# The second half of an mLSTM's token-major values through five PSUM banks instead of two

## The chip, the cores and the metric

One core of a Trainium2 chip (trn2) runs the whole kernel in one launch. The metric is the time of one execution in device microseconds (us), as the median of several runs. The engines are named as the profile names them: PE is TensorE (matmuls; PEld its weight loads), DVE VectorE, ACT ScalarE, POOL GpSimd, SP the engine that issues most DMAs (SPq is its queue). Every engine works through its instructions in the order in which they are put down for it and waits on semaphores.

## What is computed

The reference is one inference step of a hybrid encoder layer over 1152 tokens: 1024 of a prompt and 8 running streams of 16 (nine tiles of 128). A pre-RMSNorm and one input projection give the mLSTM's q, k, v and gates, the attention's q, k, v and gate, and two merge gates. Cut to what matters here:

```python
z = jnp.einsum("btd,de->bte", h, w_in) + b_in
points = [int(p) for p in np.cumsum(IN_WIDTHS)[:-1]]
mq, mk, mv, mo, mz, mi, mf, ... = jnp.split(z, points, axis=-1)
qk = silu(causal_conv(mq, mk))          # q and k of the mLSTM
v = mv.reshape(B, T, M_HEADS, M_HEAD_DIM)   # four heads of 128
h_m = chunkwise mLSTM of q, k, v and the gates, then RMSNorm
u_m = einsum(h_m * silu(mz), w_bm); u_a = einsum(h_a * silu(az), w_ba)
x + einsum(sigmoid(gm) * u_m + sigmoid(ga) * u_a, w_out)
```

The change concerns `v` of heads 2 and 3, the second half of `mv`.

## The kernel before

Every projection is a product of float32 operands split into a rounded high part and a rest, so each step along the 1024 inputs is three matmuls: high by high, high by low and low by high (`mm3`, lines 113 to 116; lines 114, 115 and 116 of the profile are all such matmuls, whatever they compute). Eight such steps (KD = 8) accumulate in one PSUM bank, 24 matmuls for a tile. Most projections are feature-major (`feature_chunk`, line 118): weights stationary, 384 tokens moving, three chunks for a tile of 128 features. The values are token-major (`mv_half`, line 230): 128 tokens stationary, 256 columns moving, one tile for each of the nine token tiles.

The eight PSUM banks of this part are two of the pool `pmain` (tag `pm`), through which all projections go in turn, and one each for the tags `mK`, `mD`, `mS`, `mB`, `mA`, `mH` of the pool `pM` (`pp`). `mK` holds the transposes of `gate_rows`; the other five are used by `mlstm_head` (lines 418 to 532).

`mv_half(1)` comes after `gate_rows()` (the exponential gates' stabilisers, small DVE and ACT work on `gscr` tiles) and `head_inputs(0)` (the projection and the causal convolution of q and k of head 0). For each token tile i it does 24 matmuls into `ps`, one DVE add of the bias into `vt` (line 243), and two DMAs of `vt` to the scratch `v_sc` in HBM (line 245). `vt` has two buffers, so the add of tile i waits until the DMAs of tile i-2 have landed; `pm` has two, so the matmuls of tile i wait for the add of tile i-2:

```python
ps = pmain.tile([P, 512], F32, tag="pm", name="pm")
for k in range(KD):
    mm3(ps[:, :n], hs(k, i), (w_hi[:, k, :n], w_lo[:, k, :n]), k == 0, k == KD - 1)
vt = m1.tile([P, 2, P], F32, tag="vt", name="vt")
dve.tensor_tensor(out=vt.rearrange("p h d -> p (h d)"), in0=ps[:, 0:256], in1=bv[:, 0:256], op=ALU.add)
for j in range(2):
    sp.dma_start(v_sc[2 * half + j][:, i, :], vt[:, j, :])
```

In the text the nine tiles of the second half are t0 to t8. After them PE goes on with `gate_unit(0)`: three chunks through `pm`, emptied by ACT into `go` (line 331). Ahead of the first of these, ACT and DVE split the eight slices of the attention's first weights (`load_wq(a["wq"][0])`, line 145 with `split`, lines 99 and 100: ACT writes `w_hi`, DVE `w_lo`), which take the place of the values' weights; their DMAs (line 144) have four buffers `wqr`.

The instructions' order on each engine is set by the framework's scheduler, which simulates a timeline when the program is built and places an instruction where the simulation finds its operands and buffers free. So DVE's order around the values mixes the adds of line 243 with the splits of weights (`wl`, line 100), the convolution of head 0 (`qT` and `kT`, line 382; silu with a table of ACT in line 384 and the product in line 385), the stabilisers (lines 294 to 324) and decay terms of head 0 that run ahead (`dx`, line 478, from `Mb`, line 420, which is read back from the scratch `M_sc`, line 319).

Of the kernel before, what the change touches and what calls it, by code (L numbers as in the profile page):

```python
# [6 lines left out]
F32 = mybir.dt.float32  # L7
# [7 lines left out]
P = 128  # L15
NT = 9
NPT = 8
T = NT * P
# [11 lines left out]
def emit(tc, a, o, ctx):  # L30
# [29 lines left out]
    pmain = keep("pmain", bufs=2, space=PSUM)  # L60
# [12 lines left out]
    ones = cp.tile([P, P], F32, name="ones")  # L73
# [15 lines left out]
    def rsqrt(y, v, t):  # L89
        """y = v ** -0.5: a guess from the exponent, then Newton steps"""  # L90
        dve.tensor_scalar(out=y.bitcast(I32), in0=v.bitcast(I32), scalar1=-0.5, scalar2=1597463007.0, op0=ALU.mult, op1=ALU.add)
        for _ in range(3):
            newton(y, v, t)
# [41 lines left out]

# [1 line left out]
    esQ, wq_ = open_pool("wq", side="right")  # L137
# [10 lines left out]

# [1 line left out]
    es0, x0 = open_pool("x0", bufs=3, side="left")  # L150
    esp0, px0 = open_pool("px0", bufs=2, space=PSUM)
    # norm_g on all partitions
    gr = x0.tile([1, 1024], F32, name="gr", bufs=1)
    sp.dma_start(gr, a["norm_g"])
    gb = px0.tile([P, 1024], F32, name="gb", bufs=1)
    for _ in range(4):  # TensorE gets up to its clock while the input arrives
        mm(gb[:, 0:P], ones, ones, start=True, stop=True)
    for q in range(2):
        mm(gb[:, q * 512:(q + 1) * 512], ones[0:1, :], gr[:, q * 512:(q + 1) * 512], start=True, stop=True)
    for i in range(NT):  # L160
# [9 lines left out]
        ss, v, r, tt = (st[:, q:q + 1] for q in range(4))  # L170
# [16 lines left out]
    def silu_evac(n, dst_of):  # L187
        """dst = silu(ps + bias) = (tanh(z / 2) + 1) * (z / 2)"""
        def ev(c, ps):
            dst = dst_of(c)  # L190
            t_ = stg.tile([P, CH], F32, tag="th", name="th")
            act.activation(out=dst, in_=ps, func=AF.Identity, scale=0.5, bias=bh[:, n:n + 1])
            act.activation(out=t_, in_=dst, func=AF.Tanh)
            dve.scalar_tensor_tensor(out=dst, in0=t_, scalar=1.0, in1=dst, op0=ALU.add, op1=ALU.mult)
        return ev

    def g_evac(j):
        """tanh(z / 2) of a merge gate (0..7 of the mLSTM branch, 8..15 of the attention branch), to scratch"""
        def ev(c, ps):
            t_ = stg.tile([P, CH], F32, tag="th", name="tg")  # L200
            act.activation(out=t_, in_=ps, func=AF.Tanh, scale=0.5, bias=bh[:, 20 + j:21 + j])
            sp.dma_start(tg_sc[j][:, c * CH:(c + 1) * CH], t_)
        return ev

# [1 line left out]
    esPS, pp = open_pool("pM", bufs=1, space=PSUM)  # L206
# [7 lines left out]
    class Scratch:  # L214
        """small tiles cut from buffers that are in use only later"""
        parts = []
# [13 lines left out]
    def mv_half(half):  # L230
        n = 264 if half == 0 else 256
        if half:
            load_wq(a["wv1"], n)
        bv = m1.tile([P, 264], F32, tag="bv", name="bv", bufs=1)
        sp.dma_start(bv[:, :n], rowb(a["bv"][264 * half:264 * half + n], n))
        if half == 0:
            mv_half.G = gscr(P, 2, 36)
        for i in range(NT):
            ps = pmain.tile([P, 512], F32, tag="pm", name="pm")
            for k in range(KD):  # L240
                mm3(ps[:, :n], hs(k, i), (w_hi[:, k, :n], w_lo[:, k, :n]), k == 0, k == KD - 1)
            vt = m1.tile([P, 2, P], F32, tag="vt", name="vt")
# [3 lines that stand above are left out]
            if half == 0:  # L246
                dve.tensor_tensor(out=mv_half.G[:, :, 4 * i:4 * i + 4], in0=ps[:, 256:264].rearrange("p (s h) -> p s h", s=2),
                                  in1=bv[:, 256:264].rearrange("p (s h) -> p s h", s=2), op=ALU.add)

    def gate_rows():  # L250
        """rows (tile, head) on partitions, tokens of the tile along the columns"""
        G = mv_half.G
# [10 lines left out]
        t1, bb, aa, A = gscr(36, P), gscr(36, P), gscr(36, P), gscr(36, P)  # L263
# [7 lines left out]
        dve.tensor_tensor_scan(out=A, data0=rs[:, 1, :], data1=aa, initial=0.0, op0=ALU.add, op1=ALU.max)  # L271
        # the running stabiliser across the chunks of the prompt: everything on one partition
        pg = pp.tile([P, 512], F32, tag="mK", name="pg")
# [20 lines left out]
        dve.tensor_copy(out=ml[0:32, :], in_=pg[0:32, 128:130])  # L294
        # the running streams: one chunk per stream
        sl = slice(32, 36)
# [8 lines left out]
        sp.dma_start(DEC, rowb(dec_sc, 64))  # L305
        # A becomes M
        pr = slice(0, 32)
# [18 lines left out]
    def gate_unit(h):  # L326
        """4 sigmoid(o) silu(z) / 2 of a head"""
        go = m1.tile([P, T], F32, tag="go", name="go", bufs=1)
# [31 lines left out]
    def conv_part(nt, out, eng):  # L360
        """out [128, T] = silu(conv(u)), the last rows of u to the conv outputs"""
        w = load_nt(a["wn"][nt], eng=pool if nt in (0, 4) else dve)
# [35 lines left out]

    # the attention part's first operands
    load_wq(a["wq"][0], CH)  # L400
# [17 lines left out]
    def mlstm_head(h, qT, kT):  # L418
# [10 lines left out]
        def state(g):  # L429
            """the memory after each chunk of the group"""  # L430
            V1 = V[g] = m2.tile([P, 3, 129], F32, tag="V1", name="V1", bufs=3)
# [114 lines left out]

# [1 line left out]
    esB, bp_ = open_pool("attnP", bufs=2, side="right")  # L548
# [3 lines left out]
    def softmax(pS, nk, bias):  # L552
        """normalised softmax of pS + bias, [128, nk]"""
        pt = ap_.tile([P, 640], F32, tag="prob", name="prob")
# [19 lines left out]
    def qk_transposes(zd):  # L574
        """psum [128, 2, 128]: q and k, the pair's two heads one after the other along the partitions"""
        px = pp.tile([P, 512], F32, tag="pX", name="pX")
        zf = zd.rearrange("p g d -> p (g d)")
        for c in range(2):
            pe.transpose(px[:, c * P:(c + 1) * P], zf[:, c * P:(c + 1) * P], ident)
        return px[:, 0:256].rearrange("p (c t) -> p c t", c=2)  # L580

    # placed in the order of first use, so that the first ones land where the mLSTM part is done first
    shapes = {"za": ([P, T], F32), "Kst": ([P, 2, TP], F32R), "Vst": ([P, NPT, 2, P], F32R),
# [39 lines left out]

    # The order of TensorE's work in this part is set here: the chains of the attention (threads) run as soon as what
    # they wait for should be there, the projections fill the time between. Times are estimates in ns; they decide
    # the order alone.
    class Line:
# [30 lines left out]
    def attend(p, i):  # L658
# [8 lines left out]
        line.now += 2 * PT_NS  # L667
        # hi and lo of a key one above the other, q twice, values as [hi | lo]
        q_hi = bp_.tile([P, 2, P], F32R, tag="q_hi", name="q_hi")
# [58 lines left out]
        for j in range(2):  # L728
# [6 lines left out]
            sPT.give(line.now)  # L735
        # sum of the four partial products of both heads, gated
        sb = ap_.tile([64, 512], F32, tag="pvs", name="pvs", bufs=1)
# [11 lines left out]

    # q of the running streams: two streams per column group, on the partitions of their keys  # L750
    QB = spl.tile([P, 2, 4, 32], F32, name="QB")
# [95 lines left out]
    def tile_work():  # L847
        """gates of the merge and, as soon as a pair's turn comes, its gate z"""
        p = 0
# [38 lines left out]

# [1 line left out]
    def load_ops(src, k0):  # L890
# [7 lines left out]
    def um_evac(j):  # L898
        """2 sigmoid(g_m) u_m, to scratch"""
        def ev(c, ps):  # L900
# [7 lines left out]
    def run_line():  # L908
        chains = [[attend(p, i) for i in range(NPT)] for p in range(4)]
        # at most two tiles of the prompt and the running streams of one pair are under way  # L910
        queue = [c for p in range(4) for c in chains[p]]
# [53 lines left out]

# [1 line left out]
    esF, fp = open_pool("fin", bufs=2, side="right")  # L967
# [3 lines left out]
    for j in range(8):  # L971
        # the projections' weights are done with
        sa = f(wq_.tile([P, KD, CH], F32R, tag=("w_hi", "w_lo")[j % 2], name="sa", bufs=1)).rearrange("p k c -> p (k c)")
# [28 lines left out]

# [1 line left out]
def layout(x):  # L1004
# [106 lines left out]
```

## Time and profile before

| | |
|---|---|
| median of 3 runs | 1077.2 us (1076.9 to 1082.35) |
| profiled execution: span from first to last instruction | 1075.1 us |
| PE busy | 1055.1 us (98%), 7078 matmuls |
| DVE / ACT / POOL busy | 658.3 / 421.3 / 241.4 us (61 / 39 / 22%) |
| mean granted PE clock | 0.998 of full speed |
| DMA | 131.58 MB, mean 122 GB/s |

Of the profiled execution the profile holds the span alone; the median is 2.1 us above it. All times in the rows below are us from the start of that span. A matmul's row gives a start and a duration; matmuls overlap in the array, so the distance from start to start is what one costs in a row of them, and the duration is longer. A row may end in brackets: how long the engine was idle before it, and what ended that.

### The profile page before, as it was taken

What the parts mean: (1) busy time and instruction counts of PE and PEld (TensorE: products, weight loads), DVE (VectorE), ACT (ScalarE), POOL (GpSimd) and SP (SyncE); (2) the same over time, 40 slices, a digit from 0 to 9 for tenths busy, and PEclk for the clock granted to TensorE, in tenths of its full rate; (3) what the DMA queues carried; (4) which work ended last, traced back from release to release, by engine and by line L of the source; (5) the groups of instructions that cost most, each with busy time, mean ns of one, the idle gap of its engine ahead of it and who ended that gap; (6) DMA issues with size and microseconds to landing.
All of it is one profiled execution on the core that took longest, in us unless ns stands there. A gap on an engine that the chain in (4) does not pass through costs nothing.

```text
span 1075.1 us, 19715 instructions
## 1 busy us (share of the span) xinstructions
PE 1055.1 (98%) x7078; PEld 1024.3 (95%) x7078; DVE 658.3 (61%) x1931; ACT 421.3 (39%) x976; POOL 241.4 (22%) x406
## 2 busy tenths in 40 slices
PE   7997999999999999999999999999999999999998
PEld 6997999999999999999999999999999999999998
DVE  6754244775847768877878688878753253573221
ACT  6441243443443215554455456544454330231100
POOL 3000000110202224434432343334322000351000
PEclk9999999999999999999999999999999999999999
DMA  8533333273523444323343244124322387663442
GB/s 241 161 88 61 101 66 53 87 121 101 116 85 127 151 146 167 117 76 111 114 126 99 62 148 137 54 71 141 111 79 84 111 262 243 202 223 106 136 143 67
DMA packets 115664, 131.58 MB, mean 122 GB/s; under 512 B 28197, under 2 KB 91885, under 8 KB 115566
## 3 DMA queue, kind: packets, MB, share of 16 engines
q1 hardware_dynamic: 108654, 120.88, 38.3%
q10 hardware_dynamic: 6912, 9.44, 2.5%
q8 instruction: 56, 0.92, 0.4%
q14 instruction: 42, 0.34, 0.1%
HBM read 96.84 MB, written 33.44 MB: 121 GB/s over the span
## 4 chain that ended last, share of the span: by engine, by line
PE 88%; DMA 6%; DVE 3%; ACT 1%; issue 1%; SPq 1%; POOL 0%; DVEq 0%; ACTq 0%
PE pm L114 24%; PE pm L116 24%; PE pm L115 24%; PE pT L570 3%; PE pv L732 3%; DMA v_sc<-vt 1%; PE pS L702 1%; PE pS L703 1%; DMA tm<-tg_sc 1%; PE pv L816 1%; DMA xt<-in_x 1%; DMA sm_sc<-tm 1%; DMA raw<-o_sc 1%; PE mA L495 1%; PE mS L477 1%
## 5 line engine op out<-in xcount | busy, mean ns | idle before, releaser
L114 PE MATMUL pm<-h_hi,wh 128*128 128x384 f32 x1056 | 357.4, 339 | 3.2 <-DVE tm L904 3.1
L116 PE MATMUL pm<-h_hi,wl 128*128 128x384 f32 x1056 | 357.5, 339 | 0.0
L115 PE MATMUL pm<-h_lo,wh 128*128 128x384 f32 x1056 | 356.9, 338 | 0.0
L114 PEld LDWEIGHTS pm<-h_hi,wh 128*128 128x128 f32 x1056 | 198.4, 188 | 8.0 <-DVE tm L904 3.2
L116 PEld LDWEIGHTS pm<-h_hi,wl 128*128 128x128 f32 x1056 | 198.3, 188 | 1.3
L115 PEld LDWEIGHTS pm<-h_lo,wh 128*128 128x128 f32 x1056 | 198.4, 188 | 0.6
L114 PE MATMUL pm<-w_hi,h_hi 128*128 128x384 f32 (+2 forms) x432 | 142.6, 331 | 8.2 <-DVE vt L243 5.4
L116 PE MATMUL pm<-w_hi,h_lo 128*128 128x384 f32 (+2 forms) x432 | 140.0, 325 | 1.2 <-DVE h_lo L100 1.2
L115 PE MATMUL pm<-w_lo,h_hi 128*128 128x384 f32 (+2 forms) x432 | 139.9, 325 | 0.0
L99 ACT ACTIVATE wh<-wr 128x512 fp32r<-128x512 f32 x104 | 65.1, 628 | 170.9 <-PE pm L115 131.8
L100 DVE TENSOR_TENSOR wl<-wr,wh 128x512 fp32r<-128x512 f32 x100 | 77.6, 776 | 68.1 <-ACT wh L99 68.0
L114 PEld LDWEIGHTS pm<-w_hi,h_hi 128*128 128x128 f32 x432 | 82.3, 191 | 13.8 <-DVE vt L243 6.0
L562 ACT ACTIVATE prob<-prob,mx 128x640 f32<-128x640 f32 (+4 forms) x72 | 51.2, 711 | 86.4 <-DVE mx L561 66.5
L116 PEld LDWEIGHTS pm<-w_hi,h_lo 128*128 128x128 f32 x432 | 82.4, 191 | 2.7 <-DVE h_lo L100 1.7
L564 POOL TENSOR_SCALAR prob<-prob,mx 128x640 f32<-128x640 f32 (+4 forms) x72 | 50.7, 704 | 150.2 <-DVE mx L563 83.7
L115 PEld LDWEIGHTS pm<-w_lo,h_hi 128*128 128x128 f32 x432 | 82.5, 191 | 0.1
L114 PE MATMUL pm<-x_hi,wh 128*128 128x384 f32 x192 | 65.1, 339 | 0.0
L116 PE MATMUL pm<-x_hi,wl 128*128 128x384 f32 x192 | 65.0, 339 | 0.0
L115 PE MATMUL pm<-x_lo,wh 128*128 128x384 f32 x192 | 65.0, 338 | 0.0
L559 DVE CUSTOM_DVE_ANT_0 prob<-pS,bias 128x640 f32<-128x640 f32 (+4 forms) x64 | 41.8, 654 | 16.6 <-PE pT L570 8.4
L981 POOL TENSOR_TENSOR sa<-sa 128x384 f32<-128x384 f32 x24 | 27.7, 1163 | 107.2 <-DVE sa L980 107.2
L994 DVE SCALAR_TENSOR_TENSOR xr<-pm,xr 128x384 f32<-128x384 f32 x24 | 13.4, 558 | 62.2 <-PE pm L116 62.2
(213 smaller groups left out, 1679.0 us busy)
## 6 DMA issues: line engine op xcount, KB each, us to landing
wr<-in_wn SPq DMA_DIRECT2D x72, 256.0 KB, 2.9
tg_sc<-tg SPq DMA_DIRECT2D x48, 192.0 KB, 1.9
kr<-in_Kc SPq DMA_DIRECT2D x16, 512.0 KB, 5.2
vr<-in_Vc SPq DMA_DIRECT2D x16, 512.0 KB, 5.2
wqr<-in_wq SPq DMA_DIRECT2D x32, 192.0 KB, 3.1
xt<-in_x SPq DMA_DIRECT2D x9, 512.0 KB, 5.3
tm<-tg_sc SPq DMA_DIRECT2D x24, 192.0 KB, 3.1
sa<-tg_sc SPq DMA_DIRECT2D x8, 576.0 KB, 4.8
```

Source lines behind the costliest of these rows:

```text
L99: act.activation(out=hi, in_=raw, func=AF.Copy)
L100: eng.tensor_tensor(out=lo, in0=raw, in1=f(hi), op=ALU.subtract)
L114: mm(ps, lhs[0], rhs[0], start=first, stop=False)
L115: mm(ps, lhs[0], rhs[1], start=False, stop=False)
L116: mm(ps, lhs[1], rhs[0], start=False, stop=last)
L559: dve.tensor_tensor_reduce(out=view, in0=pS, in1=bias, scale=1.0, scalar=-3e38, op0=ALU.add, op1=ALU.max, accum_out=mx[:, 0:1])
L562: act.activation(out=pt[:, :nk], in_=pt[:, :nk], func=AF.Exp, bias=mx[:, 1:2], accum_out=mx[:, 2:3])
L564: pool.tensor_scalar(out=pt[:, :nk], in0=pt[:, :nk], scalar1=mx[:, 3:4], scalar2=1.0, op0=ALU.mult, op1=ALU.mult)
L570: pe.transpose(pT[:, n * P:(n + 1) * P], pt[:, n * P:(n + 1) * P], ident)
L732: mm(pv[:, j * 256:(j + 1) * 256], at("Vst")[:, i + 1 - nb + n, j, :], st[:, n].rearrange("p a q -> p (a q)"), start=n == 0, stop=n == nb - 1)
L981: pool.tensor_tensor(out=sm[:, s], in0=sm[:, s], in1=ta[:, s], op=ALU.add)
L994: dve.scalar_tensor_tensor(out=xr, in0=ps.rearrange("p (i t) -> p i t", i=3), scalar=0.5, in1=xr, op0=ALU.mult, op1=ALU.add)
```

## The change

One line of `mv_half`. For the second half the nine tiles take the tags `mD`, `mS`, `mB`, `mA`, `mH`, `mD`, `mS`, `mB`, `mA` of `pM`, one bank each, in place of the two of `pm`; their name is now `pv`. The first half is unchanged. The rest of the diff takes out comments. The new line stands one line lower, so every line number after it is larger by one in the changed kernel.

```diff
         for i in range(NT):
-            ps = pmain.tile([P, 512], F32, tag="pm", name="pm")
+
+            ps = pp.tile([P, 512], F32, tag=("mD", "mS", "mB", "mA", "mH")[i % 5], name="pv") if half else pmain.tile([P, 512], F32, tag="pm", name="pm")
             for k in range(KD):
```

The scheduler builds another order around it. POOL and SP keep theirs. On PE, in the second chunk of head 0's k projection and by the stabilisers' transposes `pg`, there stood before:

```order
L114 MATMUL pm<-h_hi,wh 128x384
L115 MATMUL pm<-h_lo,wh 128x384
L291 MATMUL pg<-ident,gscr 32x1
L292 MATMUL pg<-ident,gscr 32x1
L116 MATMUL pm<-h_hi,wl 128x384
```

and now:

```order
L114 MATMUL pm<-h_hi,wh 128x384
L115 MATMUL pm<-h_lo,wh 128x384
L114 MATMUL pv<-w_hi,h_hi 128x256
L115 MATMUL pv<-w_lo,h_hi 128x256
L292 MATMUL pg<-ident,gscr 32x1
L293 MATMUL pg<-ident,gscr 32x1
L116 MATMUL pm<-h_hi,wl 128x384
```

The first two matmuls of t0 now come early, ahead of two transposes; t0's other 22 stay behind the chunk after, and the four transposes of line 322 (323 now) stand 9 matmuls later than before.

On DVE, where the stabilisers (`gscr`) and the convolution of q (`qT`) of head 0 are interleaved, there stood before:

```order
L294 COPY gscr<-pg 32x2
L382 SCALAR_TENSOR_TENSOR qT<-u,cw,qT 128x1024
L308 TENSOR_SCALAR gscr<-gscr 32x128
L313 TENSOR_SCALAR gscr<-gscr 32x128
L382 SCALAR_TENSOR_TENSOR qT<-u,cw,qT 128x128
L382 SCALAR_TENSOR_TENSOR qT<-u,cw,qT 128x1024
L311 TENSOR_SCALAR gscr<-gscr 32x128
L315 TENSOR_TENSOR gscr<-gscr 36x128
```

and now:

```order
L383 SCALAR_TENSOR_TENSOR qT<-u,cw,qT 128x1024
L295 COPY gscr<-pg 32x2
L383 SCALAR_TENSOR_TENSOR qT<-u,cw,qT 128x128
L383 SCALAR_TENSOR_TENSOR qT<-u,cw,qT 128x1024
L309 TENSOR_SCALAR gscr<-gscr 32x128
L314 TENSOR_SCALAR gscr<-gscr 32x128
```

The copy out of `pg` now stands behind the first step of the convolution, and the stabiliser rows that `M_sc` is stored from (line 308, 309 now) behind one step more. Further on, one split `wl` moves ahead of the decay terms `dx`; the adds of line 243 stand as before: the first behind `dx` and the second `wl`, the third ahead of the silu of k, then five, four splits `w_lo`, and the last.

## Rows read from the trace of the kernel before

**Rows 1.** The page: busy time of PE, share of the span, instructions.

```profile
PE 1055.1 (98%) x7078; PEld 1024.3 (95%) x7078; DVE 658.3 (61%) x1931; ACT 421.3 (39%) x976; POOL 241.4 (22%) x406
```

**Rows 2.** Windows: length, busy us and instructions by engine, granted clock, DMA share, GB/s.

```profile
78.90:97.55 18.65, 12.45 (x98) 11.67 (x97) 10.25 (x21) 6.33 (x11) 0.39 (x2) 1.00 0.46 69
97.55:101.55 4.00, 4.00 (x21) 4.00 (x22) 1.54 (x2) 0.00 (x0) 0.00 (x0) 0.57 0.23 66
...
113.54:1075.10 961.56, 954.41 (x6410) 930.92 (x6408) 592.73 (x1767) 373.38 (x869) 227.86 (x377) 1.00 0.40 121
```

**Rows 3.** PE's waits from 78 to 100 us: total, times, longest.

```profile
PE pm L114 <- DVE vt L243: 5.4, 3, 3.4
PE pm L114 <- ACT u L370: 0.8, 1, 0.8
```

**Rows 4.** PE's timeline: start, duration, engine, line, operation, out and in, [idle before].

```profile
78.55 0.33 PE L115 MATMUL pm<-h_lo,wh 128*128 128x384 f32 x1
78.72 0.34 PE L116 MATMUL pm<-h_hi,wl 128*128 128x384 f32 x1
79.88 0.39 PE L114 MATMUL pm<-w_hi,h_hi 128*128 128x256 f32 x1 [0.82 <-ACT u L370]
...
97.55 0.39 PE L114 MATMUL pm<-w_hi,h_hi 128*128 128x256 f32 x1 [3.43 <-DVE vt L243]
...
101.54 0.28 PE L116 MATMUL pm<-w_hi,h_lo 128*128 128x256 f32 x1
...
113.42 0.28 PE L116 MATMUL pm<-w_hi,h_lo 128*128 128x256 f32 x1
113.54 0.34 PE L114 MATMUL pm<-h_hi,wh 128*128 128x384 f32 x1
```

**Rows 5.** The chain of waits from 76 to 98 us: start, duration, what.

```profile
76.86 6.71 DMA Mb<-M_sc
...
87.51 9.43 DMA v_sc<-vt
```

**Rows 6.** DVE's timeline around the adds of the values.

```profile
86.38 0.42 DVE L243 TENSOR_TENSOR vt<-pm,bv 128x256 f32<-128x256 f32 x1
...
90.51 0.42 DVE L243 TENSOR_TENSOR vt<-pm,bv 128x256 f32<-128x256 f32 x1
...
97.07 0.42 DVE L243 TENSOR_TENSOR vt<-pm,bv 128x256 f32<-128x256 f32 x1 [4.68 <-DMA v_sc<-vt]
97.41 1.35 DVE L385 SCALAR_TENSOR_TENSOR kT<-sg,kT 128x1152 f32<-128x1152 f32 x1
98.67 0.42 DVE L243 TENSOR_TENSOR vt<-pm,bv 128x256 f32<-128x256 f32 x1
```

**Rows 7.** DVE's timeline at the stabilisers, 67 to 72 us.

```profile
67.93 0.15 DVE L294 COPY gscr<-pg 32x2 f32<-32x2 f32 x1 [0.97 <-PE pg L292]
68.39 1.28 DVE L382 SCALAR_TENSOR_TENSOR qT<-u,cw,qT 128x1024 f32<-128x1024 f32 x1 [0.32 <-ACT qT L380]
69.60 0.27 DVE L308 TENSOR_SCALAR gscr<-gscr 32x128 f32<-32x128 f32 x1
...
69.99 1.53 DVE L382 SCALAR_TENSOR_TENSOR qT<-u,cw,qT 128x128 f32<-128x128 f32 x2
```

**Rows 8.** DMA issues: count, KB each, us to landing. The values' from 97 to 115 us, then t1's.

```profile
v_sc<-vt SPq DMA_DIRECT2D x14, 64.0 KB, 1.6
...
v_sc<-vt SPq DMA_DIRECT2D x2, 64.0 KB, 6.0
```

**Rows 9.** ACT's timeline at the first chunk of the gate, then SP's DMAs for its weights.

```profile
117.04 1.01 ACT L99 ACTIVATE w_hi<-wqr 128x384 fp32r<-128x384 f32 x2 [1.14 <-DMA wqr<-in_wq]
117.96 0.56 ACT L331 ACTIVATE go<-pm,bh 128x384 f32<-128x384 f32 x1
...
112.36 1.76 SPq L144 DMA_DIRECT2D wqr<-in_wq  x4
```

**Rows 10.** First use of the banks by a head: min/median/max ns, first and last start us.

```profile
L477 PE MATMUL mS<-qT,kT x72: 270/275/276, 143.1 to 342.8; 128*128 128x128 f32 x72
```

## The prediction

> **What bounds the kernel.** I read the page first: PE is busy for 1055.1 of 1075.1 us [rows 1], so only what keeps PE from its next matmul can move the time, and at most 20 us are to be had. Then the windows by stage: from 113.54 us to the end PE idles for 961.56 - 954.41 = 7.2 us in all at full clock, while from 78.90 to 97.55 it idles for 18.65 - 12.45 = 6.2 us, and in the 4 us after that the granted clock is 0.57 of full, so mostly the lower of its two levels, 1.2 instead of 2.4 GHz [rows 2]. That stretch is exactly the second half of the values. PE's waits say on what: three times on the add of line 243 that empties `pm` (5.4 us, the longest 3.4) and once on line 370, which empties the last convolution chunk but one out of the same two banks (0.8 us) [rows 3]. All four are waits for a bank. The chain of waits says why the longest is so long: `Mb` lands 6.71 us after its issue, DVE's `dx` stands in front of the first add, and the DMAs of t0 then take 9.43 us to land [rows 5]. Since `vt` has two buffers, the add of t2 waits for them until 97.07 [rows 6]; since `pm` has two, t4 waits for that add and starts at 97.55 [rows 4].
>
> **What the stretch costs.** At full clock the value matmuls follow each other at (113.42 - 101.54) / 99 = 0.120 us (99 steps lie between those two rows) [rows 4]. Nine tiles of 24 are 216 matmuls, 25.92 us. The last matmul of the chunk before starts at 78.72, and these follow each other at 78.72 - 78.55 = 0.17, so t0 could start at 78.90; the gate's first chunk starts at 113.54 [rows 4]. The stretch takes 34.64 us, so 34.64 - 25.92 = **8.7 us** are lost. Of these 1.0 us stand ahead of t0 (79.88 instead of 78.90). From 97.55 to 101.54 lie 20 matmuls in 3.99 us where 2.40 would do, 1.6 us for the low clock and the restart. The rest, 6.1 us, are the three waits of 5.4 us and the restarts after them.
>
> **The change, part by part.** (a) *t0's bank.* `mD` has not been used since this part began, so t0 no longer waits for line 370: -1.0 us. Two of its matmuls move ahead of the transposes of line 291, which costs the chunk there 2 x 0.12 = 0.24 us and saves as much later: zero.
>
> (b) *Banks for t1 to t8.* t1 to t4 have fresh banks and wait for nothing. t5 to t8 need the banks of t0 to t3. With PE unbroken, t0's other 22 matmuls start at 78.90 + 0.24 = 79.14, and each tile takes 24 x 0.12 = 2.88 us: t4 ends at 93.3, t5 starts there, t6 at 96.2, t7 at 99.06, t8 at 101.94, and the end is 79.14 + 214 x 0.12 = 104.82. The adds of t0 to t3 ended at 86.8, 90.9, 97.5 and 99.1 before [rows 6], so t5 has 6.5 us of room, t6 5.3, t7 **1.6**, t8 2.8. If the adds stay where they are, all three waits go: 104.82 instead of 113.54. Without an idle spell of 3.4 us the clock has no reason to fall, which is in the 8.7.
>
> (c) *The adds do not quite stay.* The new order on DVE puts one convolution step ahead of the copy from `pg` and another ahead of line 308. The copy goes from 67.93 to about 69.6, behind the step that starts at 68.39; the two steps of together 1.53 us follow, so line 308 runs at 69.75 + 1.53 = 71.3 instead of 69.60: 1.7 us later [rows 7]. `M_sc` is stored from it, `Mb` is read back from `M_sc`, `dx` waits for `Mb`, and t0's add stands behind `dx`: t0's add slips from 86.38 to 88.1 at worst. With the 9.43 us its DMAs would land 1.7 us later too, and t2's add would end at 97.5 + 1.7 = 99.2, against t7's start at 99.06: 0.1 us. From the other side, one split `wl` now stands ahead of `dx`, so SP issues the weights' DMA and the stores of the convolution's last rows ahead of the values' earlier, and t0's writes may land sooner than before; a wait of 0 then. I take 0, since the upper bound is 0.1. t3's add comes behind the silu of 1.35 us [rows 6] at 99.2 + 1.35 + 0.4 = 101.0, still ahead of t8 at 101.94.
>
> (d) *What is late next.* The adds of t4 to t7 are no longer paced by PE but by `vt`: an add of 0.42 [rows 6], two issues (0.9, by the 1.76 us of four issues in [rows 9]) and the landing, 1.6 in this stretch [rows 8], together 2.9 us for a turn of one of its two buffers. t2's add ends at 99.2 at the latest, so t4's starts at 101.7 and t6's at 104.6; t3's ends at 101.0, so t5's starts at 103.5 and t7's at 106.4. Behind it on DVE stand the four splits `w_lo`, which free the buffers `wqr` for the next four weight DMAs; in the trace the last `w_hi` on ACT ends 118.05 - 112.36 = 5.7 us after the first of these DMAs [rows 9]. So ACT comes to line 331 at some 106.8 + 5.7 = 112.5 and is done at 113.1. PE needs that bank for the gate's third chunk, after two chunks of 24 x 0.17 = 4.1 us: 104.82 + 8.2 = 113.0. The two meet: 0 to 1 us. I take 0, as these times all start from the late bound of (c).
>
> (e) *The heads.* `mS` and the others are first used by a head at 143.1 us [rows 10], 30 us after the values' end, so the new sharing of banks adds no wait there.
>
> **The sum.** -8.7 us on the span: 1075.1 - 8.7 = 1066.4. What follows on PE stands in the same order, and its idle 7.2 us in 961 belong to chains that start from PE's own results, so the shift lasts to the end. The median stands 2.1 us above the profiled span; 1077.2 - 8.7 = **1068.5 us**, 0.8% less. A change under 0.5% (5.4 us) could hardly be told from none here.
>
> **Rivals.** *A, given back at the gate.* If the writes of `vt` take 6.0 us to land, as t1's did [rows 8], a buffer's turn is 7.3 us: t4 and t5 are added at 106 and 108, t6 and t7 at 113 and 115, the last `w_hi` ends at 121, line 331 at 122, and PE waits 9 us for the gate's third chunk. Everything would be given back there: 1077. For it: SP's queue holds the same stores in the same order, and 9.43 and 6.0 us were seen [rows 5, 8]. Against it: those writes were queued behind a weight load and the convolution's stores, the later ones took 1.6. Half of it (a landing of 3 to 4 us) gives 1071 to 1074. 10% and 12%.
>
> *B, slower: the clock stays low through the values.* The end of the stretch would be 79.14 + 214 x 0.20 = 121.9 at the pitch of the slow 20 matmuls (3.99 / 20), 8.4 us later than now: 1085.6. It ends slower once more than (34.4 - 25.7) / 0.08 = 109 of the 214 matmuls run so. Against it: with two banks, two idle spells between tiles of 5.4 - 3.4 = 2.0 us together [rows 3] left the clock at 1.00 from 78.90 to 97.55 [rows 2]; it fell only behind the spell of 3.43 [rows 4], and with five banks I find no spell at all. 4%.
> By the Trainium skill, "TensorE: Matmul & The Clock Gate", section "A second HAM failure mode: psum-queue depth-cycling", a kernel that goes through PSUM banks in turn lets PE idle so often between its groups of matmuls that the clock keeps changing between its levels. By that rule rotating over five banks would be rival B; rows 2 speak against it.
>
> *C, the change doesn't do what it says.* The waits would be bank releases in name only, and each place would at once be taken by another (for the weights' split, or for the normed input): 1077. Against it: all four waits end with an operation that empties `pm` [rows 3], and weights and input were used by earlier matmuls of the same tiles. 4%.
>
> **Chances.** The forecast, all or nearly all of the 8.7 us, 1066 to 1071: 70%. Half given back: 12%; A: 10%; B: 4%; C: 4%. The range of 1066.0 to 1074.0 us takes in the 0 to 1 us of (d) and the half, and leaves out A, B and C. Faster by over 0.5% (under 1071.8): 0.76; within 0.5%: 0.19; slower: 0.05.
>
> **What would show it.** Right: PE's waits hold no `pv` behind line 244 of the changed kernel; the gate's first chunk starts at 104.8; the clock is 1.00 from 79 to 114. (c) is right if t0's add comes at 87 to 88 and t2's ends near 99. (d) is wrong if PE waits for line 332 at the third chunk. The prediction is wrong if t7 or t8 waits for more than 1 us, or if a wait of several us appears after 115 us that is not in the present trace.

## The result and the profile after

| | before | changed |
|---|---|---|
| median, first comparison (4 runs each) | 1079.78 us | 1068.12 us (1066.71 to 1069.30) |
| ratio, 95% interval | | 0.9891 [0.9868, 0.9915] |
| profiled execution: span | 1075.1 us | 1065.6 us |
| PE busy | 1055.1 us | 1052.3 us |
| stage of the values, from the first matmul that could follow the convolution's chunk to the gate's first | 34.64 us | 25.92 us |

The change is faster; the forecast of 1068.5 us and its range hold the time. One run of the kernel before in a later comparison, of 1724.37 us at a mean granted clock of 0.56, is left out of every median here. The profile of the changed kernel shows PE's waits behind 76 us, and none is left on the add of the values, now line 244, nor on a bank that a convolution chunk holds (before: [rows 3]):

```profile
PE pm L114 <- DVE tm L905: 1.1, 3, 0.5
PE pm L114 <- ACT tg L201: 0.7, 1, 0.7
PE pm L114 <- DVE zt L606: 0.3, 1, 0.3
PE mH L523 <- POOL num L520: 0.2, 1, 0.2
```

PE's timeline at both ends of the stage (before: [rows 4]):

```profile
79.60 0.33 PE L116 MATMUL pm<-h_hi,wl 128*128 128x384 f32 x1
79.77 0.28 PE L116 MATMUL pv<-w_hi,h_lo 128*128 128x256 f32 x1
...
105.33 0.29 PE L116 MATMUL pv<-w_hi,h_lo 128*128 128x256 f32 x1
105.45 0.34 PE L114 MATMUL pm<-h_hi,wh 128*128 128x384 f32 x1
```

t0 follows the chunk at its pitch, and 214 matmuls take 105.45 - 79.77 = 25.68 us, 0.120 each; with the two that moved ahead (0.24 us) 25.92. The windows of the stretch, in the columns of [rows 2], have PE and its weight loads busy throughout and the clock at full:

```profile
78.90:97.55 18.65, 18.65 (x155) 18.65 (x155) 10.57 (x21) 7.33 (x12) 0.79 (x2) 1.00 0.48 78
97.55:101.55 4.00, 4.00 (x36) 4.00 (x35) 1.91 (x4) 0.00 (x0) 0.00 (x0) 1.00 0.36 99
```

Of the 9.5 us between the two spans, 34.64 - 25.92 = 8.72 are this stage. This execution reached the chunk's end later, 79.60 instead of 78.72, of which 0.24 are the two matmuls and 0.64 lie in the first 62 us, where nothing was changed; and from the gate to the end it took 960.15 instead of 961.56 us. Both are within what executions of one kernel differ by: in three profiles of the kernel before (two of them below) the last matmul of the chunk starts at 78.72 to 81.08 us, and from the gate to the end it takes 959.8 to 961.6 us.

DVE's timeline (before: [rows 6, 7]) shows steps (c) and (d): the stabiliser's row, the `dx`, then t0's, t2's, t3's and t7's adds.

```profile
69.06 1.28 DVE L383 SCALAR_TENSOR_TENSOR qT<-u,cw,qT 128x1024 f32<-128x1024 f32 x1 [1.44 <-ACT qT L381]
70.26 0.14 DVE L295 COPY gscr<-pg 32x2 f32<-32x2 f32 x1
...
71.79 0.27 DVE L309 TENSOR_SCALAR gscr<-gscr 32x128 f32<-32x128 f32 x1
...
84.48 1.67 DVE L479 SCALAR_TENSOR_TENSOR dx<-Mb,TOK,cmask 128x128 f32<-128x128 f32 x6 [1.58 <-DMA Mb<-M_sc]
...
86.66 0.42 DVE L244 TENSOR_TENSOR vt<-pv,bv 128x256 f32<-128x256 f32 x1
...
96.75 0.42 DVE L244 TENSOR_TENSOR vt<-pv,bv 128x256 f32<-128x256 f32 x1 [4.86 <-DMA v_sc<-vt]
...
98.36 0.42 DVE L244 TENSOR_TENSOR vt<-pv,bv 128x256 f32<-128x256 f32 x1
...
103.85 0.43 DVE L244 TENSOR_TENSOR vt<-pv,bv 128x256 f32<-128x256 f32 x1 [1.52 <-PE pv L116]
```

t2's add still waits for t0's writes, until 96.75: the slow writes are there as before, and only PE no longer hangs on them. t7 reaches t2's bank at 79.77 + 22 x 0.12 + 6 x 2.88 = 99.7, 2.5 us after that add's end.

### The profile page after: what moved, and what is told of

Its sections match the earlier page's. It is cut to its first block, busy times and chain, and to the rows that moved or that the text cites. A ratio compares the mean times of both kernels' runs of the same rounds, so it can differ in the third digit from the quotient of the medians.

```text
span 1065.6 us, 19714 instructions
## 1 busy us (share of the span) xinstructions
PE 1052.3 (99%) x7078; PEld 1023.0 (96%) x7078; DVE 657.4 (62%) x1931; ACT 421.4 (40%) x976; POOL 242.5 (23%) x406
## 4 chain that ended last, share of the span: by engine, by line
PE 88%; DMA 5%; DVE 4%; issue 1%; ACT 1%; POOL 1%; SPq 0%; DVEq 0%; POOLq 0%; ACTq 0%
PE pm L114 24%; PE pm L116 23%; PE pm L115 23%; PE pT L571 3%; PE pv L733 3%; DMA sm_sc<-tm 1%; PE pS L703 1%; PE pS L704 1%; DMA xt<-in_x 1%; PE pv L817 1%; PE pv L115 1%; PE pv L116 1%; PE pv L114 1%; DMA V<-v_sc 1%; PE pS L792 1%
## 5 line engine op out<-in xcount | busy, mean ns | idle before, releaser
L114 PE MATMUL pm<-w_hi,h_hi 128*128 128x384 f32 (+1 forms) x360 | 121.1, 337 | 3.1 <-ACT h_hi L99 1.8
L116 PE MATMUL pm<-w_hi,h_lo 128*128 128x384 f32 (+1 forms) x360 | 119.0, 332 | 1.2 <-DVE h_lo L100 1.2
L115 PE MATMUL pm<-w_lo,h_hi 128*128 128x384 f32 (+1 forms) x360 | 118.8, 331 | 0.0
L114 PEld LDWEIGHTS pm<-w_hi,h_hi 128*128 128x128 f32 x360 | 68.3, 190 | 7.7 <-issue 4.1
L116 PEld LDWEIGHTS pm<-w_hi,h_lo 128*128 128x128 f32 x360 | 68.0, 189 | 2.7 <-DVE h_lo L100 1.7
L115 PEld LDWEIGHTS pm<-w_lo,h_hi 128*128 128x128 f32 x360 | 68.2, 190 | 0.1
```

Source lines behind the costliest of these rows:

```text
L114: mm(ps, lhs[0], rhs[0], start=first, stop=False)
L115: mm(ps, lhs[0], rhs[1], start=False, stop=False)
L116: mm(ps, lhs[1], rhs[0], start=False, stop=last)
```

## The experiments

Three theories were tested. *Banks*: PE lost its time to tiles that waited for a bank which a late add had not emptied. *Order*: the gain is the new order of the instructions, which came with the change. *Writes*: what matters is that the adds wait for the DMAs of `vt`. In all but one of the six altered kernels every engine's order is that of the kernel it is made from, so each changes waits alone. Times of one comparison stand beside the same runs of the kernel before (1079.14 us for the first four, 1079.97 for the next three).

**Three banks, in the order of the changed kernel.**

```diff
-tag=("mD", "mS", "mB", "mA", "mH")[i % 5]
+tag=("mD", "mS", "mB")[i % 3]
```

> Three banks for the nine tiles (mD, mS, mB in turn) instead of five; every engine's order is that of the changed kernel. Theory 'banks' (PE lost its time to tiles waiting for a bank that an add had not yet emptied): t5 comes round to t2's bank. PE would reach t5 at 93.9 us, t2's add ends at 97.2, so one wait of 3.3 us on line 244, and if the granted clock falls behind it as in the kernel before, 1.6 us more; no other tile waits. The gate's first chunk starts at 108.7 (clock kept) to 110.3 (clock fallen) instead of 105.45, and the time is 3.3 to 4.9 us above the changed kernel's 1068.1: 1071.4 to 1073.0. Rival 'order' (the gain is the new order of DVE, ACT and PE around the values, the banks hardly count): same time and same start of the gate as the changed kernel.

1073.36 us, ratio 0.9948 [0.9933, 0.9963]; the changed kernel with more `vt` buffers (below), whose stage is that of the changed kernel, took 1070.43 in the same comparison. PE's timeline has the one wait that was expected, at t5, then DVE's the add of t2 that ends it:

```profile
96.69 0.38 PE L114 MATMUL pv<-w_hi,h_hi 128*128 128x256 f32 x1 [2.07 <-DVE vt L244]
```

```profile
96.22 0.42 DVE L244 TENSOR_TENSOR vt<-pv,bv 128x256 f32<-128x256 f32 x1 [3.81 <-DMA v_sc<-vt]
```

The stage is 108.31 - 80.30 = 28.01 us, 2.3 more than 25.68. So *order* falls as the whole cause: with the order intact, two banks fewer cost 2.3 us in the stage and 2.9 in the time. In the stage the size is below the expected 3.3 to 4.9: this execution came to t5 later and t2's add was earlier, and the clock stayed full. In the time it is not settled: against the changed kernel's own ratios, 0.9891 and 0.9899, the loss is 5 to 6 us. The profile is of the fastest run, 1069.95 us at a mean clock of 1.0; the other five ran at 0.998 and 1072.8 to 1074.5, so in those the clock fell somewhere; whether it fell behind this wait, no profile here shows.

**Two banks, but of the heads' pool.**

```diff
+tag=("mD", "mS")[i % 2]
```

> Two banks, but mD and mS of the heads' pool instead of the two that all projections share. The order of DVE, ACT, POOL and SP is that of the changed kernel; on PE six matmuls of the gate's first chunk move ahead of t3. Theory 'banks': only the wait ahead of t0 (line 370, 1.0 us) is gone for certain. t2 waits for t0's add 1.8 us, t3 not at all, since the six gate matmuls fill it, t4 waits for t2's add 3.3 us, and the clock falls once, 1.6 us: 6.7 us above the changed kernel, 1074.8, some 2 us below the kernel before. Rival 'sharing' (the harm was that values and projections share two banks, not their number): no wait on line 244 beyond 1 us, 1068 to 1070. Rival 'order': 1068.

1073.66 us, ratio 0.9947 [0.9932, 0.9962]. PE waits at t2 and t4:

```profile
87.49 0.38 PE L114 MATMUL pv<-w_hi,h_hi 128*128 128x256 f32 x1 [1.58 <-DVE vt L244]
...
96.70 0.38 PE L114 MATMUL pv<-w_hi,h_hi 128*128 128x256 f32 x1 [2.12 <-DVE vt L244]
```

The stage is 111.19 - 80.23 = 30.96 us, less 6 x 0.17 for the gate's matmuls in it 29.9, 4.2 above the changed kernel's. *Sharing* falls as the whole cause: with two banks, separate ones leave two waits. It lost less than expected, since the clock was full in the profile, but the scheduler, which sees a wait coming, also put gate work into it; this is the one kernel with an order of its own.

Yet 1079.14 - 1073.66 = 5.5 us, half of the gain, are had here with two banks: t0's wait for line 370 is gone, gate work stands ahead of t3, and t4's wait is shorter, with no fall of the clock in the profile. Part of this is probably the order: with two buffers `vt`, t2's add starts 16.1 to 17.3 us behind the chunk's last matmul in the five profiles of the changed order (96.22 - 80.06 = 16.2 here), and 18.4 to 20.2 in the three of the order before (97.07 - 78.72 = 18.4 in the first). Five banks in the order before were not run, so how the gain divides between banks and order stays open.

**The kernel before with four buffers `vt`.**

```diff
-tag="vt", name="vt")
+tag="vw" if half and i % 4 > 1 else "vt", name="vt")
```

> The kernel before with its two banks, and four buffers instead of two for the values behind the add (vt) in the second half; every engine's order is that of the kernel before. Theory 'banks, with a write behind the longest wait': t2's add no longer waits for the writes of t0 (9.43 us to land), so it ends near 92.8, t4 does not wait, and the clock does not fall: 3.6 + 1.6 = 5.2 us of the 8.7 go; the waits of t0, t2 and t3 (1.0, 1.1, 1.1 us) stay. Time 1077.2 - 5.2 = 1072.0, gate's first chunk at about 108.3 instead of 113.54. Rival 'DVE's place' (t2's add is late for its place in DVE's order, behind the convolution of k, and not for the writes): same as before, 1077.

1073.33 us, ratio 0.9946 [0.9930, 0.9962]. PE's waits in the stage, then DVE's add of t2:

```profile
81.76 0.39 PE L114 MATMUL pm<-w_hi,h_hi 128*128 128x256 f32 x1 [1.38 <-ACT u L370]
...
88.41 0.39 PE L114 MATMUL pm<-w_hi,h_hi 128*128 128x256 f32 x1 [0.63 <-DVE vt L243]
...
92.53 0.39 PE L114 MATMUL pm<-w_hi,h_hi 128*128 128x256 f32 x1 [0.99 <-DVE vt L243]
```

```profile
93.85 0.42 DVE L243 TENSOR_TENSOR vt<-pm,bv 128x256 f32<-128x256 f32 x1
```

The longest wait, t4's, is gone, and with it the fall of the clock; t0's, t2's and t3's are left. So the writes were behind the longest wait and behind that one alone: from the same order as before, 1079.14 - 1073.33 = 5.8 us are had without a single new bank.

**The changed kernel with four buffers `vt`** (the same edit).

> The changed kernel with four buffers vt; every engine's order is that of the changed kernel. Theory 'banks': with five banks PE waits for no add any more, so earlier adds are worth nothing: t2's add ends near 92.7 instead of 97.2, the gate's first chunk starts at 105.4 as before, time 1068.1 (within 2 us). Rival 'writes still pace the stretch': the gate's first chunk comes earlier and the time falls by over 2 us.

1070.43 us, ratio 0.9916 [0.9901, 0.9932]. t2's add comes 4.5 us earlier than in the changed kernel, and PE takes 106.24 - 80.56 = 25.68 us for the 214 matmuls, as before:

```profile
92.25 0.42 DVE L244 TENSOR_TENSOR vt<-pv,bv 128x256 f32<-128x256 f32 x1
```

Once no tile waits for an add, an earlier add is worth nothing. The time is 2.3 us above 1068.1, just outside the 2 us expected; the intervals of the two ratios overlap, so a loss is not shown, and a gain is not there. Banks and buffers cure the same wait; the banks cure the other three too.

**The changed kernel once more.**

> The changed kernel itself, once more beside the kernel before. The forecast was 8.7 us less, the first comparison gave 11.7 between the medians and 9.5 between the profiled spans, the stage of the values 8.7. If the stage is the whole effect: 8.0 to 10.0 us between the medians here (0.9907 to 0.9926), the gate's first chunk 25.7 us behind the first value matmul of the long run. If something outside the stage gains too: 11 to 12 us again, and a second stage of the profile is shorter by 2 to 3 us than in the kernel before.

1068.47 us against 1079.97, ratio 0.9899 [0.9881, 0.9916]; the stage is 107.66 - 81.98 = 25.68 us. So the time falls by some 11 us, reliably more than the 8.7 of the stage in the two first profiles. No other stage is shorter by 2 to 3 us. The question that this left is taken up below. This run's mean clock is 0.998, but the fall is elsewhere, some 40 us ahead of the stage, as its window shows:

```profile
36.10:39.50 3.40, 3.40 (x16) 3.40 (x17) 2.98 (x6) 0.62 (x3) 0.00 (x0) 0.50 0.66 205
```

So a mean clock alone does not say where it fell.

**Four banks.**

```diff
+tag=("mD", "mS", "mB", "mA")[i % 4]
```

> Four banks (mD, mS, mB, mA in turn), every engine's order that of the changed kernel. Theory 'banks': t6 comes round to t2's bank, PE reaches it 17 us behind the start of the values (at 96.8 in the changed kernel's trace) and t2's add ended between 96.6 and 97.2 in three traces: a wait of 0 to 0.4 us, nothing else. Stage of the values 25.7 to 26.2 us, time within 1 us of the changed kernel beside it. If every bank counted alike (two to five banks gave 8.7 us, so some 2.9 a bank), it would be 2 to 3 us slower than the changed kernel.

1068.26 us, ratio 0.9905 [0.9887, 0.9923], the time of the changed kernel; no wait on line 244, stage 105.30 - 79.42 = 25.88 us. PE's last matmul of t5 and first of t6, then DVE's add of t2, whose bank t6 takes:

```profile
96.33 0.29 PE L116 MATMUL pv<-w_hi,h_lo 128*128 128x256 f32 x1
96.56 0.39 PE L114 MATMUL pv<-w_hi,h_hi 128*128 128x256 f32 x1
```

```profile
96.08 0.43 DVE L244 TENSOR_TENSOR vt<-pv,bv 128x256 f32<-128x256 f32 x1 [4.76 <-DMA v_sc<-vt]
```

PE could have started t6 at 96.45 and starts it 0.1 us later, just behind the add's end at 96.51. The fifth bank is hardly worth anything, but the fourth only just suffices. Banks don't count by number: from the third to the fourth the stage gains 28.01 - 25.88 = 2.1 us, because PE comes to t2's bank about when its late add ends, and from the fourth to the fifth 0.2.

**Five banks and a single buffer `vt`.**

```diff
-tag="vt", name="vt")
+tag="vw" if half else "vt", name="vt", bufs=1 if half else 2)
```

> Five banks, but a single buffer behind the add (vt) in the second half; every engine's order is that of the changed kernel. It makes the writes pace the adds, as rival A had it. Theory 'given back at the gate': t1's add waits for t0's writes, to 96.8, and each later one follows 2.9 us behind the one before; t7's add comes at 114, so DVE's first four splits of the attention's weights, their next DMAs, ACT's splits and then line 332 come 10 us late, and PE, which passes the values with less than 1 us of waits and reaches the gate's third chunk at 114, waits there for 7 us, with a fall of the clock behind it (1.6 us): 8 to 9 us over the changed kernel, 1077. If ACT's place behind the weights doesn't bind (another order of events frees the bank): within 1 us of the changed kernel.

1077.55 us, ratio 0.9982 [0.9966, 0.9999]: 9.1 us above the changed kernel. The values pass in 105.29 - 78.98 = 26.31 us, hardly longer, and PE then waits at the gate's third chunk. DVE's add of t7, ACT's line 332 and PE's matmul, one timeline each:

```profile
111.68 0.42 DVE L244 TENSOR_TENSOR vt<-pv,bv 128x256 f32<-128x256 f32 x1 [2.15 <-DMA v_sc<-vt]
```

```profile
118.68 1.03 ACT L332 ACTIVATE go<-pm,bh 128x384 f32<-128x384 f32 x2
```

```profile
119.30 0.69 PE L114 MATMUL pm<-h_hi,wh 128*128 128x384 f32 x1 [5.49 <-ACT go L332]
```

This is the path of rival A: adds that are paced by the writes hold back the split of the next weights, that holds back ACT, and the wait comes up in another stage. The wait is 5.5 us instead of the expected 7, since each add follows 2.6 us behind the one before and not 2.9. The clock falls during the wait and stays low for 3.3 us behind it, as two windows show, the wait and the time after it:

```profile
113.80:119.30 5.50, 0.01 (x2) 0.01 (x1) 2.65 (x6) 2.56 (x6) 0.00 (x0) 0.68 0.80 232
119.30:122.60 3.30, 3.30 (x10) 3.30 (x11) 0.07 (x1) 0.42 (x1) 0.00 (x0) 0.50 0.42 130
```

In the changed kernel the same path has 2 us to spare (next section).

**The kernel before, profiled twice more**, for the 11 us. In 27 runs of it beside the experiments the time goes with the mean granted clock: median 1077.8 us at 0.998 (6 runs), 1079.6 at 0.997 (13), 1080.1 at 0.996 (4), 1082.6 at 0.995 (4). The profile ahead of the prediction is of a run at 0.998, and its span lies 1.8 us under 1076.9, the fastest time of the three, the distance that every later profile has to its own time.

> The kernel before, profiled once more. Its runs beside the others go from 1076.4 to 1083.6 us, and their mean granted clock from 0.998 to 0.995; the first profile was of a run at the low end (0.998). Theory 'longer fall': behind the wait of 3.4 us ahead of t4 the clock stays at its lower level longer in most runs than the 3.4 us of the first profile, so a profile of a run with a clock of 0.997 or less shows a lower clock for some 7 us from about 98 us, and a stage of the values of 36 us instead of 34.6. Rival 'elsewhere': the stage is 34.6 again and the difference lies in the first 60 us or in the last 200.

> The same kernel, a third profile, for a second draw from the same spread: 'longer fall' expects the stage's length to go with the run's mean clock (34.6 us at 0.998, 36 at 0.996 to 0.997, more below), 'elsewhere' expects it at 34.6 whatever the clock.

1081.39 and 1078.13 us, both at a clock of 0.997. The first one's waits, then its windows from the fall of the clock to t4's start, from there to its rise, and the whole from 100 to 110 us, then both ends of its stage with t4, then the second one's t4:

```profile
PE pm L114 <- DVE vt L243: 6.7, 3, 4.8
```

```profile
100.00:101.33 1.33, 0.00 (x0) 0.00 (x0) 0.47 (x2) 0.00 (x0) 0.00 (x0) 0.58 0.52 75
101.33:107.00 5.67, 5.67 (x26) 5.67 (x27) 1.69 (x3) 0.00 (x0) 0.00 (x0) 0.50 0.16 46
100.00:110.00 10.00, 8.66 (x51) 8.67 (x52) 2.56 (x5) 0.00 (x0) 0.00 (x0) 0.66 0.22 52
```

```profile
81.08 0.34 PE L116 MATMUL pm<-h_hi,wl 128*128 128x384 f32 x1
...
101.33 0.58 PE L114 MATMUL pm<-w_hi,h_hi 128*128 128x256 f32 x1 [4.79 <-DVE vt L243]
...
118.33 0.34 PE L114 MATMUL pm<-h_hi,wh 128*128 128x384 f32 x1
```

```profile
99.57 0.58 PE L114 MATMUL pm<-w_hi,h_hi 128*128 128x256 f32 x1 [4.65 <-DVE vt L243]
```

In both, t4 waits 4.7 to 4.8 us instead of 3.4, and the clock stays low for 6.8 us instead of 3.4 (0.34 of 10 us, at half speed); of these 6.8 us 1.1 and 1.2 lie in the wait itself, ahead of t4's start. The stages are 118.33 - 81.25 = 37.1 and 116.51 - 79.09 = 37.4 us (each start is the chunk's last matmul and 0.17), over 1 us more than the 36 expected. Against 25.9 that is 11.2 and 11.5 us lost, about the whole of the measured gain. *Elsewhere* falls as a cause, and *longer fall* holds in part. Of the 2.5 and 2.8 us that are lost beyond the first profile's 8.7, some 1.4 and 1.8 are longer waits for the banks and their restarts, and about 1.0 the longer stretch at the low clock. Runs at 0.995 and 0.996 were not profiled. What differs between 1081.39 and 1078.13 lies outside the stage: the chunk's end at 81.08 or 78.92 accounts for 2.2 us of it.

## Why the prediction was right, and where it was off

*What bounds it and the loss* held. The stretch can be done in 25.92 us and is; all four waits of [rows 3] are gone, and the clock with them at 1.00. In the profile that the sum was made on, the term of 8.7 us is met to within 0.1 (34.64 to 25.92).

*The size of the step "the sum"* is what was off: it took one execution's loss for the median's. Median against median the kernel gained 11.7 and 11.5 us. The profiled execution was the mildest of the three profiled: the wait ahead of t4 was 3.4 us in it and 4.7 to 4.8 in the next two, and the low clock lasted half as long. The forecast said that the profile holds the span alone and put the 2.1 us up to the median down as a fixed distance; it was 1.8 us of distance and a run faster than the median. 1068.5 was met all the same, and that is luck: 1077.2 was a low median too, 2 to 3 us under the later ones, and the two errors cancel.

*(a) t0's bank*: right. The two early matmuls stand at 68.25 and 68.36 and the chunk's end moved by the 0.24. The gate's first chunk starts at 105.45 and not 104.8, by the 0.64 us that this execution started later.

*(b) Banks for t5 to t8*: right, no wait. That four banks do does not follow from the forecast's numbers: with four, t6 at 96.2 would need the bank of t2, whose add was to end at 97.5. It took an add that ends earlier, which the run with four showed.

*(c) The adds slip*: the delay is there, but it does not reach the adds, so by the forecast's own sign (t0's add at 87 to 88, t2's end near 99) the step is wrong. The row that `M_sc` is stored from moved from 69.60 to 71.79, by 1.5 when the later start of 0.65 is taken off. But t0's add came at 86.66, 0.3 us later than before and, with the start taken off, earlier, and t2's ended at 97.2, 2 us ahead of the bound. The six `dx` now run without the split `wl` between them, so t0's add starts 2.2 us behind the first of them and not 2.8, which the step left out; and `M_sc` was written faster, as SP's timeline shows: `M_sc` stored at 72.08, `Mb` issued behind its landing at 77.97, 5.9 us later, where the row before took 7.0 (69.89 to 76.86).

```profile
72.08 0.31 SPq L320 DMA_DIRECT2D M_sc<-gscr  x1
...
77.97 0.37 SPq L421 DMA_DIRECT2D Mb<-M_sc  x1
```

*(d) What is late next*: right in kind, with more room than forecast. ACT's timeline (before: [rows 9]):

```profile
110.02 1.02 ACT L99 ACTIVATE w_hi<-wqr 128x384 fp32r<-128x384 f32 x2 [1.27 <-DMA wqr<-in_wq]
110.94 0.56 ACT L332 ACTIVATE go<-pm,bh 128x384 f32<-128x384 f32 x1
```

Line 332 is done at 111.5, not 113.1, and PE wants the bank at 105.45 + 48 x 0.173 = 113.75: 2 us to spare, because the adds of t4 to t7 came at 99.3 to 103.85, up to 2.5 us ahead of the estimate. They are paced by `vt`, as forecast, though the row of t7's add (103.85) names PE: t7's last matmul had started at 102.45, over a us before. In the second profile of the changed kernel the same add waits for a landing:

```profile
106.26 0.42 DVE L244 TENSOR_TENSOR vt<-pv,bv 128x256 f32<-128x256 f32 x1 [1.54 <-DMA v_sc<-vt]
```

In the run with one buffer t7's add comes 111.68 - 103.85 = 7.8 us later than here; less the 2.25 us to spare (113.75 - 111.5), that is about the wait of 5.5 us.

*(e) The heads*: right, no new wait at the heads; the one of 0.2 us on `mH` stands in both later profiles of the kernel before too.

*Rivals.* A did not happen here, but its mechanism is real. B, the low clock by rotation, did not: the clock was 1.00 over all of 78 to 118 us in the three profiles with five banks and at least two buffers `vt`. The price it was given is a little low: at the low clock the value matmuls follow each other at 0.21 us and not 0.20, since the 20 matmuls it was read from held some at full clock. The Trainium skill ("TensorE: Matmul & The Clock Gate", section "A second HAM failure mode: psum-queue depth-cycling") tells of a kernel whose PE idles between its groups of matmuls so often that the clock keeps changing. These rows do not test that: with five banks PE had no wait in the stage. C did not happen.

Open is why t0's writes take 9 us or more to land. They are queued behind a weight load and the stores of the convolution's last rows, which land 9 to 10 us after their own issue. The forecast that t0's writes may land sooner came true: the new order issues these stores at 82.88 to 83.35 us, some 4 us ahead of t0's writes (85.22 to 85.69 before, under 2 us ahead), and with two buffers t2's add, which waits for t0's writes, starts 9.0 to 10.2 us behind t0's in five profiles of the new order, and 10.7 to 12.0 in three of the old. That fits the queue, but moving the stores alone was not tried.

## What to carry to other kernels

A wait for a bank is worth what stands behind the late release: count, for each tile, which earlier tile's evacuation it needs, and give just as many banks as carry PE past the latest one; one more gained 0.2 us here. Banks that a later stage owns are free until its first use. Before a sum is made from one profile, see where its execution lies among the runs and whether the mean clock differs between them: here the wait and the fall of the clock cost 8.7 us in a fast run and 11.2 and 11.5 us in two others.

## What the runs showed of the hardware

The lower clock did not last as long every time, nor begin at the same place. With a wait of 3.4 us it began 0.5 us behind the wait's end and lasted 3.4 us; with waits of 4.65, 4.8 and 5.5 us it lasted 6.8 us and began 1.1 to 3.5 us before the wait ended. It did not come in the stage in the profiled runs whose longest waits were 2.07 and 2.12 us. It also came without a long wait: in the second profile of the changed kernel, behind two waits of 0.80 and 0.75 us, from 36.1 to 39.5 us.

At the lower clock, matmuls of 256 columns followed each other at 0.21 us instead of 0.12, as two rows of the kernel before, profiled a second time, show; 13 steps lie between them:

```profile
102.14 0.42 PE L114 MATMUL pm<-w_hi,h_hi 128*128 128x256 f32 x1
...
104.92 0.41 PE L115 MATMUL pm<-w_lo,h_hi 128*128 128x256 f32 x1
```

There PE worked through 5.7 us of the low clock, some 27 matmuls (5.7 / 0.21), each 0.09 longer: about 2.5 us on top of the wait of 4.8.

The spread is smaller without the waits: the kernel before ran from 1076.4 to 1083.6 us (over 30 runs), the changed one from 1066.7 to 1070.2 (8 runs, and fewer runs show less spread).
